# One Trainium2 core, one hybrid encoder layer: weights in column tiles from the host, and a fold without transposes

## The chip, the core and the metric

The kernel runs on one core of one Trainium2 chip. Its engines are TensorE (PE, with its weight loads PEld), VectorE (DVE), ScalarE (ACT), GpSimd (POOL) and SyncE (SP), which issues nearly all DMAs from one queue in order. The metric is the time of one execution on the device in microseconds (us); lower is better. A time is the median of a few runs. The profile is one execution of its own.

## The reference

One encoder layer on x of 2048 tokens by 1024, all in float32, with 256 memory tokens. Three sub-layers, each between two RMS norms:

```python
u = rms_norm(h, g_mix_pre);  z = u @ w_in                       # 1024 x 2816
ya = swa_with_sinks(qa, ka, va, sinks)                          # 8 heads of 64, window of chunks
yh = hgrn2(qh, fh, ih, gh, lb, onorm)                           # 4 heads of 128, gated recurrence
h = h + rms_norm(concat(ya, yh) @ w_out, g_mix_post)
u = rms_norm(h, g_x_pre);  m = rms_norm(mem, g_mem)
q, k, v = u @ wq, m @ wk, m @ wv                                # 4 heads of 256
h = h + rms_norm(softmax(q @ k.T / 16) @ v @ wo, g_x_post)
u = rms_norm(h, g_ffn_pre)
h = h + rms_norm((silu(u @ w_gate) * (u @ w_up)) @ w_down, g_ffn_post)   # 1024 x 2816, 2816 x 1024
```

## The kernel before

A float32 product is made from two parts of each operand in the type fp32r: hi, a rounded copy, and lo, what is left (raw - hi). Three matmuls stand for one: hi*hi, hi*lo, lo*hi (`mm3`, and `products` at L1002 to L1004). So every weight tile that is loaded (a raw tile) is first split: one copy makes hi and one subtraction on DVE makes lo. For the tiles of the `wp` pool this is `split`: hi on POOL at L142, lo on DVE at L143. `raw_tile` and `split_tiles` allot them, two buffers for each of raw, hi and lo, and `wcols` loads a block of 128 columns of a weight and splits it. A raw tile is 128 x 1024, 512 KB.

The stages, in the order of time:

- `in_first` projects the first half of the tokens with w_in; the weights stream through `streamed` (tiles `sraw`, in `in_block` two loads of 128 columns each for a half of the rows).
- `in_proj` / `in_cols` projects the second half, a block of 128 columns at a time (`wcols` of w_in), interleaved with `swa` and `hgrn` for the first half, whose input comes back from the DRAM tensor `z_d`.
- `fold_cross`, interleaved with the last `hgrn` blocks (L776 to L834 are theirs). It multiplies the cross-attention weights with the memory tokens once: k from w_k (`projected`, 8 tiles, 24 matmuls of 256 columns each), then for each of 8 row blocks of w_q the product with k (24 matmuls of 256 columns; the result is `qk_d`), then v from w_v (as k), then the product of v with w_o (8 tiles, 12 matmuls of 512 columns each; the result is `vo_d`). A row block of w_q has its model rows on the partitions and is needed the other way round: `transpose_split` transposes it on PE in eight blocks of 128 x 128 (L124) into two PSUM banks, which ACT and DVE take over as hi and lo (L126, L127). The other three weights go through `split`. PSUM banks here are of four kinds, g, t, s and h, two buffers each; the fold uses s and h.
- `phases` runs the rest from a list of jobs: out-projection (`mixed_block`), scores and values of the cross-attention, the FFN's gate and up (`hidden_blocks`, weights streamed with 256 columns a load) and down. Its products are 2 x 2 block products of seven multiplications instead of eight where the block's kind is "s"; `resident` prepares the operands T, `streamed` the operands S. Residual rows are added by DMAs that POOL issues (`add`, L1348); their descriptors lie in a ring in SBUF, whose size the program sets (`dynamic_dma_scratch_size`).

A scheduler in the build decides the order of the instructions on each engine from its own model of times; the engines then run their queues in order, and SP its DMAs. An instruction that waits holds up all behind it on its engine.

Of the kernel before, what the change touches and what calls it, by code (L numbers as in the profile page):

```python
# [24 lines left out]
KT = D // P  # L25
# [11 lines left out]
def f32(ap):  # L37
    return ap.bitcast(F32)
# [10 lines left out]
class Layer:  # L49
# [24 lines left out]
    def load(self, dst, src):  # L74
        self.nc.sync.dma_start(dst, src)
# [52 lines left out]

    def raw_tile(self):
        self._n += 1  # L130
        return self.wp.tile([P, D], F32, tag="raw", name=f"raw_{self._n}", bufs=2)

    def split_tiles(self):
        self._n += 1
        hi = self.wp.tile([P, D], F32R, tag="hi", name=f"whi_{self._n}", bufs=2)
        lo = self.wp.tile([P, D], F32R, tag="lo", name=f"wlo_{self._n}", bufs=2)
        return hi, lo

    def split(self, raw, hi, lo, lo_engine=None):

        nc = self.nc
        nc.gpsimd.tensor_scalar(hi, raw, 1.0, 1.0, ALU.mult, ALU.mult)  # L142
        (lo_engine or nc.vector).tensor_tensor(lo, raw, f32(hi), ALU.subtract)  # L143

    def wcols(self, w, c0, lo_engine=None):

        raw = self.raw_tile()
        self.load(raw.rearrange("p (k c) -> p k c", k=KT), w[:, c0:c0 + P].rearrange("(k p) c -> p k c", p=P))
        hi, lo = self.split_tiles()
        self.split(raw, hi, lo, lo_engine)  # L150
# [112 lines left out]
    def fold_cross(self):  # L263

        nc, ph = self.nc, self.xp
        gx = ph.tile([P, KT], F32, name="gx")
        self.load(gx, self.I["g_x_pre"].rearrange("r (k p) -> p (r k)", p=P))
        nc.vector.tensor_scalar_mul(gx, gx, float(M) ** -0.5)
        g = self.gain(self.I["g_mem"])
        mT = [ph.tile([P, KT, M], F32R, name=f"mT{i}") for i in range(2)]  # L270
        raw_tile, split_tiles = self.raw_tile, self.split_tiles

        def projected(w):
            dst = [ph.tile([P, KT, M], F32R, tag=f"kv{i}", name=f"kv{i}_{self._n}") for i in range(2)]
            for j in range(KT):
                wh, wl = self.wcols(w, j * P)
                ps = self.bank("sh"[j % 2])[:, :M]
                self.mm3(ps, [((wh[:, k, :], wl[:, k, :]), (mT[0][:, k, :], mT[1][:, k, :])) for k in range(KT)])
                nc.scalar.activation(dst[0][:, j, :], ps, AF.Copy)
                nc.vector.tensor_tensor(dst[1][:, j, :], ps, f32(dst[0][:, j, :]), ALU.subtract)  # L280
                yield dst

        for t in range(M // P):
            m = raw_tile()
            self.load(m, self.I["mem"][t * P:(t + 1) * P, :])
            u = self.pre_norm(m, g)
            self.transpose_split(u, lambda q: mT[0][:, 4 * q:4 * q + 4, t * P:(t + 1) * P],
                                 lambda q: mT[1][:, 4 * q:4 * q + 4, t * P:(t + 1) * P])
        for kT in projected(self.I["wk_x"]):
            yield  # L290
        for d in range(KT):
            wq = raw_tile()
            self.load(wq, self.I["wq_x"][d * P:(d + 1) * P, :])
            th, tl = split_tiles()
            th = th.rearrange("p (k c) -> p k c", k=KT)
            tl = tl.rearrange("p (k c) -> p k c", k=KT)
            self.transpose_split(wq, lambda q: th[:, 4 * q:4 * q + 4, :], lambda q: tl[:, 4 * q:4 * q + 4, :])
            o = self.io_tile("x")
            for q in range(2):
                ps = self.bank("sh"[q])  # L300
                for r in range(2):
                    h = 2 * q + r
                    self.mm3(ps[:, r * M:(r + 1) * M],
                             [((th[:, j, :], tl[:, j, :]), (kT[0][:, j, :], kT[1][:, j, :])) for j in (2 * h, 2 * h + 1)])
                sl = slice(q * 512, (q + 1) * 512)
                nc.scalar.activation(o[:, sl], ps, AF.Copy, scale=gx[:, d:d + 1])
            self.store(self.qk_d[d * P:(d + 1) * P, :], o)
            yield
        for vT in projected(self.I["wv_x"]):
            yield  # L310
        for h in range(4):
            banks = [[self.bank(k) for k in "sh"] for _ in range(2)]
            for i in range(2):
                j = 2 * h + i
                raw = raw_tile()
                self.load(raw, self.I["wo_x"][j * P:(j + 1) * P, :])
                wh, wl = split_tiles()
                self.split(raw, wh, wl)
                for mt in range(2):
                    ms = slice(mt * P, (mt + 1) * P)  # L320
                    ah, al = vT[0][:, j, ms], vT[1][:, j, ms]
                    for q in range(2):
                        sl = slice(q * 512, (q + 1) * 512)
                        nc.tensor.matmul(banks[mt][q], ah, wh[:, sl], start=(i == 0), stop=False)
                        nc.tensor.matmul(banks[mt][q], ah, wl[:, sl], start=False, stop=False)
                        nc.tensor.matmul(banks[mt][q], al, wh[:, sl], start=False, stop=(i == 1))
# [189 lines left out]
    def in_block(self, ca, cb, beside, get, between):  # L516

        nc, w = self.nc, self.I["w_in"]
        z, x = [], []

        def load(t, j):
            if between and j:
                between()
            for i, c in enumerate((ca, cb)):
                self.load(t[:, :, i * P:(i + 1) * P], w[j * 512:(j + 1) * 512, c * P:(c + 1) * P]
                          .rearrange("(k p) c -> p k c", p=P))

        def stream(kind):
            for n in beside:
                t = self.pair_tile()  # L530
                self.load(t[:, 0, :], self.I["x"][TB + n * P:TB + (n + 1) * P, :])
                x.append((n, t))
            for _ in range(3):
                next(iter(get), None)
            return self.streamed(load, 4, kind)

        def out(i, j, a, b):
            if not z:
# [19 lines left out]
        def after():  # L558
# [29 lines left out]
    def in_cols(self, b, u, cols, e1):  # L588
        nc = self.nc
        w = []  # L590
        for c in cols:
            w.append(self.wcols(self.I["w_in"], c * P))
# [20 lines left out]
        for i, c in enumerate(cols):  # L613
            c0 = c * P
# [269 lines left out]
    def resident(self, get, nk, key, dst, keep, sums):  # L884
# [70 lines left out]
    def streamed(self, load, nk, kind, engine=None):  # L955

        nc = self.nc
        raw = []
        for j in range(2):
            self._n += 1  # L960
            t = self.ts.tile([P, 4, 256], F32, tag="raw", name=f"sraw_{self._n}", bufs=self.raws)[:, :nk, :]
            load(t, j)
            raw.append(t)
        yield None
        a11, a21 = raw[0][:, :, 0:P], raw[0][:, :, P:2 * P]
        a12, a22 = raw[1][:, :, 0:P], raw[1][:, :, P:2 * P]

        def made(src, e):
            self._n += 1
# [523 lines left out]
    def down_block(self, c, f0, nk, n):  # L1493
# [51 lines left out]
        def after():  # L1545
# [44 lines left out]
```

## Time and profile before

| | before |
|---|---|
| runs | 2653.74, 2656.38, 2657.7 us, median 2656.38 |
| the profiled execution | span 2652.4 us from its first to its last instruction; the median of the runs is 4.0 us above it |
| PE busy | 2568.9 us, 97% of the span |
| DVE, ACT, POOL busy | 1714.9, 1240.2, 485.2 us |
| DMA | 494.48 MB, 186 GB/s on average |
| granted TensorE clock | 0.990 on average |

A busy PE is not PE at its peak: matmuls overlap, and their ends are modelled, so the distance between the starts of two of them says what one costs. In the windows below, the columns are the stretch, its length, then busy time and (instructions) of PE, PEld, DVE, ACT and POOL, the granted clock, the share of the 16 DMA engines and GB/s. The chain of waits gives start, length and what. A row of the waits gives who waited for whom, us in total, times, and the longest. A row of a tile gives shortest / median / longest in ns and the first and last start.

### The profile page before, as it was taken

To read this page: it belongs to the slowest core of one execution; us is meant where nothing else is said; L and a number is where in the kernel's file an instruction comes from. 1 tells how busy PE (TensorE), PEld (TensorE's weight loads), DVE (VectorE), ACT (ScalarE), POOL (GpSimd) and SP (SyncE) were. 2 spreads that over 40 slices of the span, in tenths; PEclk is the share of its full clock that TensorE was granted. 3 is DMA by queue.
4 is the path that set the end of the run, shared out by engine and by line. 5 is a ranking of instruction groups with operands and counts; after the bars stand their busy time and mean duration, and the time that the engine had idled before them with its cause. 6 is when DMAs were issued, how large, how long until landed. Compare 5 with 4: busy or idle time off the path is not lost.

```text
span 2652.4 us, 34824 instructions
## 1 busy us (share of the span) xinstructions
PE 2568.9 (97%) x12329; PEld 2145.1 (81%) x12329; DVE 1714.9 (65%) x2701; ACT 1240.2 (47%) x2604; POOL 485.2 (18%) x675
## 2 busy tenths in 40 slices
PE   7999999999988999999989999999999999999998
PEld 6877888888986877888878888888888888888886
DVE  7675578877545657777666655556666656564656
ACT  5463366655433556555564333344333334353543
POOL 4240344322432323223310000000000000001022
PEclk9999999999999999999999999999999999999999
DMA  5435655445877998676893633253566435576988
GB/s 183 144 130 165 191 156 159 131 140 171 233 234 222 276 296 266 210 238 176 220 307 126 192 120 95 80 182 127 168 198 211 162 108 171 173 232 173 264 214 215
DMA packets 405102, 494.48 MB, mean 186 GB/s; under 512 B 20416, under 2 KB 311232, under 8 KB 404928
## 3 DMA queue, kind: packets, MB, share of 16 engines
q1 hardware_dynamic: 394272, 453.46, 53.3%
q0 software_dynamic: 10656, 38.80, 8.3%
q8 instruction: 97, 1.59, 0.2%
q14 instruction: 77, 0.63, 0.1%
HBM read 333.85 MB, written 158.33 MB: 186 GB/s over the span
## 4 chain that ended last, share of the span: by engine, by line
PE 75%; DMA 10%; issue 7%; DVE 4%; POOL 3%; ACT 2%; SPq 0%; POOLq 0%; DVEq 0%; ACTq 0%
PE psm L1002 20%; PE psm L1004 20%; PE psm L1003 20%; PE psg L160 2%; PE psg L159 2%; PE psg L158 2%; PE pss L1237 1%; DMA row<-y_d 1%; DMA row<-in_w_out_dram 1%; DMA u_d<-row 1%; DMA raw<-in_wv_x_dram 1%; DMA raw<-in_wo_x_dram 1%; DVE wlo L143 1%; DMA row<-in_x_dram 1%; DMA pair<-in_x_dram 0%
## 5 line engine op out<-in xcount | busy, mean ns | idle before, releaser
L1002 PE MATMUL psm<-T,S 128*128 128x512 f32 x2699 | 1049.2, 393 | 19.9 <-ACT part L1017 6.9
L1003 PE MATMUL psm<-T,S 128*128 128x512 f32 x2699 | 1054.7, 391 | 5.7 <-DVE T L880 5.7
L1004 PE MATMUL psm<-T,S 128*128 128x512 f32 x2699 | 1046.4, 392 | 0.7 <-DVE S L880 0.6
L1002 PEld LDWEIGHTS psm<-T,S 128*128 128x128 f32 x2699 | 509.3, 189 | 132.3 <-ACT part L1017 8.2
L1003 PEld LDWEIGHTS psm<-T,S 128*128 128x128 f32 x2699 | 509.3, 189 | 111.8 <-DVE T L880 7.4
L1004 PEld LDWEIGHTS psm<-T,S 128*128 128x128 f32 x2699 | 509.2, 189 | 108.9 <-DVE S L880 3.1
L880 DVE TENSOR_TENSOR S<-sraw,S 128x512 fp32r<-128x512 f32 (+1 forms) x320 | 222.9, 703 | 213.3 <-ACT S L877 195.9
L877 ACT ACTIVATE S<-sum 128x512 fp32r<-128x512 f32 (+1 forms) x310 | 186.4, 619 | 342.5 <-PE psm L1004 244.3
L880 DVE TENSOR_TENSOR S<-sum,S 128x512 fp32r<-128x512 f32 (+1 forms) x368 | 248.5, 686 | 55.4 <-ACT S L877 35.7
L1017 ACT ACTIVATE part<-psm 128x512 f32<-128x512 f32 x270 | 160.0, 597 | 245.9 <-PE psm L1004 227.9
L1348 POOL DMA_DIRECT2D row<-y_d x28 | 25.7, 918 | 1127.4 <-DVE row L1521 1033.9
L877 ACT ACTIVATE S<-sraw 128x512 fp32r<-128x512 f32 (+1 forms) x273 | 168.0, 616 | 122.7 <-PE psm L1004 102.8
L880 DVE TENSOR_TENSOR T<-row,T 128x1024 fp32r<-128x1024 f32 (+1 forms) x122 | 144.2, 1195 | 63.8 <-ACT T L877 63.6
L158 PE MATMUL psg<-u,whi 128*128 128x512 f32 x352 | 141.3, 401 | 1.6 <-POOL whi L142 1.6
L160 PE MATMUL psg<-u,wlo 128*128 128x512 f32 x352 | 139.6, 397 | 0.9 <-DVE wlo L143 0.9
L159 PE MATMUL psg<-u,whi 128*128 128x512 f32 x352 | 139.4, 396 | 0.0
L877 ACT ACTIVATE T<-row 128x1024 fp32r<-128x1024 f32 x122 | 122.3, 1028 | 33.2 <-DVE row L906 17.9
L1319 ACT ACTIVATE junk<-row 128x512 f32<-128x512 f32 x160 | 99.9, 626 | 79.1 <-DVE row L1341 28.4
L879 POOL TENSOR_SCALAR S<-sum 128x512 fp32r<-128x512 f32 x58 | 50.2, 865 | 209.8 <-PE psm L1004 159.9
L977 DVE TENSOR_TENSOR sum<-sraw,sraw 128x512 f32<-128x512 f32 (+1 forms) x92 | 64.0, 696 | 32.0 <-DMA sraw<-h1t_d 8.7
L143 DVE TENSOR_TENSOR wlo<-raw,whi 128x1024 fp32r<-128x1024 f32 x46 | 60.3, 1311 | 36.1 <-POOL whi L142 36.1
L1472 DVE TENSOR_TENSOR row<-psm,part 128x512 f32<-128x512 f32 x63 | 41.7, 688 | 59.3 <-PE psm L1004 59.2
(332 smaller groups left out, 3622.0 us busy)
## 6 DMA issues: line engine op xcount, KB each, us to landing
sraw<-in_w_gate_dram SPq DMA_DIRECT2D x44, 512.0 KB, 3.9
sraw<-in_w_up_dram SPq DMA_DIRECT2D x44, 512.0 KB, 4.0
hid_d<-row SPq DMA_DIRECT2D x44, 512.0 KB, 2.6
h_d<-row SPq DMA_DIRECT2D x32, 512.0 KB, 5.8
y_d<-row SPq DMA_DIRECT2D x32, 512.0 KB, 3.1
sraw<-hid_d SPq DMA_DIRECT2D x32, 512.0 KB, 5.3
row<-h_d POOLq DMA_DIRECT2D x30, 512.0 KB, 6.5
row<-u_d SPq DMA_DIRECT2D x30, 512.0 KB, 6.3
```

Source lines behind the costliest of these rows:

```text
L143: (lo_engine or nc.vector).tensor_tensor(lo, raw, f32(hi), ALU.subtract)
L158: nc.tensor.matmul(ps, ah, bh, start=(i == 0), stop=False)
L159: nc.tensor.matmul(ps, ah, bl, start=False, stop=False)
L160: nc.tensor.matmul(ps, al, bh, start=False, stop=(i == n - 1))
L877: self.nc.scalar.activation(hi, raw, AF.Copy)
L880: self.nc.vector.tensor_tensor(lo, raw, f32(hi), ALU.subtract)
L977: nc.vector.tensor_tensor(t, a, b, op)
L1002: nc.tensor.matmul(ps, s[:, 0, k, :], t[:, 0, k, :], start=st, stop=False, **kw)
L1003: nc.tensor.matmul(ps, s[:, 0, k, :], t[:, 1, k, :], start=False, stop=False, **kw)
L1004: nc.tensor.matmul(ps, s[:, 1, k, :], t[:, 0, k, :], start=False, stop=sp, **kw)
L1017: nc.scalar.activation(t, ps, AF.Copy)
L1319: self.nc.scalar.activation(junk, a, AF.Square, scale=float(D) ** -0.5, accum_out=to)
```

## The change

- The host lays six weights (w_in, w_q, w_k, w_v, w_gate, w_up) out in tiles of 128 columns: tile c holds, for each partition, all eight row blocks of these columns in one run of 4 KB. w_q is transposed first. A raw tile of `wcols` is then one contiguous block of 512 KB; before, it was read in runs of 512 B. The streamed loads of w_in and of w_gate and w_up read runs of 2 KB; before, 512 B and 1 KB.
- In the fold, w_q goes through `wcols` like w_k, and its transposes and their take-over are gone.
- raw, hi and lo of the `wp` pool have three buffers instead of two. To make room for them, POOL's descriptor ring gets 2048 B of a partition instead of the default.
- `split` takes the engine of hi; in the fold hi is made by ACT (`"A"`), in the in-projection and for k of the attention still by POOL.

```diff
 def raw_tile:      tag="raw",   -bufs=2  +bufs=3
 def split_tiles:   tag="hi","lo" -bufs=2  +bufs=3
-    def split(self, raw, hi, lo, lo_engine=None):
+    def split(self, raw, hi, lo, engine="P"):
-        nc.gpsimd.tensor_scalar(hi, raw, 1.0, 1.0, ALU.mult, ALU.mult)
-        (lo_engine or nc.vector).tensor_tensor(lo, raw, f32(hi), ALU.subtract)
+        if engine == "A":
+            nc.scalar.activation(hi, raw, AF.Copy)
+        else:
+            nc.gpsimd.tensor_scalar(hi, raw, 1.0, 1.0, ALU.mult, ALU.mult)
+        nc.vector.tensor_tensor(lo, raw, f32(hi), ALU.subtract)
 def wcols:
-        self.load(raw.rearrange("p (k c) -> p k c", k=KT), w[:, c0:c0 + P].rearrange("(k p) c -> p k c", p=P))
+        self.load(raw, w[c])
 def fold_cross:
-                wh, wl = self.wcols(w, j * P)
+                wh, wl = self.wcols(w, j, "A")
-            wq = raw_tile()
-            self.load(wq, self.I["wq_x"][d * P:(d + 1) * P, :])
-            th, tl = split_tiles()
...
-            self.transpose_split(wq, lambda q: th[:, 4 * q:4 * q + 4, :], lambda q: tl[:, 4 * q:4 * q + 4, :])
+            th, tl = self.wcols(self.I["wq_x"], d, "A")
-                self.split(raw, wh, wl)
+                self.split(raw, wh, wl, "A")
 def in_block:
-                self.load(t[:, :, i * P:(i + 1) * P], w[j * 512:(j + 1) * 512, c * P:(c + 1) * P]
-                          .rearrange("(k p) c -> p k c", p=P))
+                self.load(t[:, i, :], w[c, :, j * 512:(j + 1) * 512])
 def streamed:  with tiled=True the two column blocks of a raw tile lie one behind the other
 def hidden_blocks:
-                t, w[j * 512:(j + 1) * 512, f * P:(f + 2) * P].rearrange("(k p) c -> p k c", p=P)), 4, kind, "A")
+                t, w[f:f + 2, :, j * 512:(j + 1) * 512].rearrange("i p d -> p i d")), 4, kind, "A", tiled=True)
+TILED = ("w_in", "wq_x", "wk_x", "wv_x", "w_gate", "w_up")
+def tiled(w):
+    return np.ascontiguousarray(w.reshape(KT, P, -1, P).transpose(2, 1, 0, 3)).reshape(-1, P, D)
 def kernel:
+        if name in TILED:
+            host[name] = tiled(host[name].T if name == "wq_x" else host[name])
-    nc = _bacc.Bacc("TRN2", target_bir_lowering=False, num_devices=1)
+    nc = _bacc.Bacc("TRN2", target_bir_lowering=False, num_devices=1, dynamic_dma_scratch_size=2048)
```

More of the change, by code (lines that the diff above doesn't have):

```diff
@@ L130, in raw_tile, with wcols @@
         self._n += 1
-        return self.wp.tile([P, D], F32, tag="raw", name=f"raw_{self._n}", bufs=2)
+        return self.wp.tile([P, D], F32, tag="raw", name=f"raw_{self._n}", bufs=3)
     def split_tiles(self):
         self._n += 1
-        hi = self.wp.tile([P, D], F32R, tag="hi", name=f"whi_{self._n}", bufs=2)
-        lo = self.wp.tile([P, D], F32R, tag="lo", name=f"wlo_{self._n}", bufs=2)
+        hi = self.wp.tile([P, D], F32R, tag="hi", name=f"whi_{self._n}", bufs=3)
+        lo = self.wp.tile([P, D], F32R, tag="lo", name=f"wlo_{self._n}", bufs=3)
         return hi, lo
-    def split(self, raw, hi, lo, lo_engine=None):
+    def split(self, raw, hi, lo, engine="P"):
         nc = self.nc
-        nc.gpsimd.tensor_scalar(hi, raw, 1.0, 1.0, ALU.mult, ALU.mult)
-        (lo_engine or nc.vector).tensor_tensor(lo, raw, f32(hi), ALU.subtract)
-    def wcols(self, w, c0, lo_engine=None):
+        if engine == "A":
[3 more added lines that the diff above has]
+        nc.vector.tensor_tensor(lo, raw, f32(hi), ALU.subtract)
+    def wcols(self, w, c, engine="P"):
         raw = self.raw_tile()
-        self.load(raw.rearrange("p (k c) -> p k c", k=KT), w[:, c0:c0 + P].rearrange("(k p) c -> p k c", p=P))
+        self.load(raw, w[c])
         hi, lo = self.split_tiles()
-        self.split(raw, hi, lo, lo_engine)
+        self.split(raw, hi, lo, engine)
         return (hi.rearrange("p (k c) -> p k c", k=KT), lo.rearrange("p (k c) -> p k c", k=KT))
@@ L291, in fold_cross @@
         for d in range(KT):
-            wq = raw_tile()
-            self.load(wq, self.I["wq_x"][d * P:(d + 1) * P, :])
-            th, tl = split_tiles()
-            th = th.rearrange("p (k c) -> p k c", k=KT)
-            tl = tl.rearrange("p (k c) -> p k c", k=KT)
-            self.transpose_split(wq, lambda q: th[:, 4 * q:4 * q + 4, :], lambda q: tl[:, 4 * q:4 * q + 4, :])
+            th, tl = self.wcols(self.I["wq_x"], d, "A")
             o = self.io_tile("x")
@@ L534, in stream @@
                 next(iter(get), None)
-            return self.streamed(load, 4, kind)
+            return self.streamed(load, 4, kind, tiled=True)
         def out(i, j, a, b):
@@ L591, in in_cols @@
         for c in cols:
-            w.append(self.wcols(self.I["w_in"], c * P))
+            w.append(self.wcols(self.I["w_in"], c))
         z = [self.io_tile("z") for _ in cols]
@@ L953, in mark, with streamed @@
             self.last[e] = next((i for i in reversed(traced) if i.engine == e), None)
-    def streamed(self, load, nk, kind, engine=None):
+    def streamed(self, load, nk, kind, engine=None, tiled=False):
         nc = self.nc
@@ L960, in streamed @@
             self._n += 1
-            t = self.ts.tile([P, 4, 256], F32, tag="raw", name=f"sraw_{self._n}", bufs=self.raws)[:, :nk, :]
-            load(t, j)
-            raw.append(t)
+            t = self.ts.tile([P, 4, 256], F32, tag="raw", name=f"sraw_{self._n}", bufs=self.raws)
+            if tiled:
+                t = t.rearrange("p k c -> p (k c)").rearrange("p (i d) -> p i d", i=2)
+                load(t, j)
+                raw.append([t[:, i, :].rearrange("p (k c) -> p k c", c=P) for i in range(2)])
+            else:
+                t = t[:, :nk, :]
+                load(t, j)
+                raw.append([t[:, :, i * P:(i + 1) * P] for i in range(2)])
         yield None
-        a11, a21 = raw[0][:, :, 0:P], raw[0][:, :, P:2 * P]
-        a12, a22 = raw[1][:, :, 0:P], raw[1][:, :, P:2 * P]
+        (a11, a21), (a12, a22) = raw
         def made(src, e):
```

## The prediction

> **What bounds the kernel now.** I read the page first (busy shares and the chain that ended last), then the windows by stage, then the chain, the waits and the DMA issues inside the one stage that the windows single out.
>
> ```profile
> span 2652.4 us, 34824 instructions
> PE 75%; DMA 10%; issue 7%; DVE 4%; POOL 3%; ACT 2%; SPq 0%; POOLq 0%; DVEq 0%; ACTq 0%
> 1500.00:1600.00 100.00, 100.00 (x443) 82.81 (x442) 58.22 (x88) 35.59 (x63) 0.00 (x0) 1.00 0.44 138
> 640.00:700.00 60.00, 54.24 (x396) 51.92 (x394) 36.84 (x47) 23.81 (x63) 25.20 (x25) 0.94 0.86 231
> 700.00:752.00 52.00, 49.39 (x410) 49.00 (x409) 21.89 (x38) 26.37 (x77) 16.57 (x23) 0.97 0.74 230
> 752.00:787.00 35.00, 26.85 (x195) 25.33 (x194) 17.43 (x24) 6.75 (x20) 14.56 (x13) 0.90 0.90 268
> 787.00:815.00 28.00, 26.00 (x124) 20.19 (x123) 11.67 (x11) 6.98 (x14) 8.41 (x8) 1.00 0.70 244
> ```
>
> The chain is 75% TensorE. The FFN window (1500 to 1600) shows what its floor is: 443 matmuls in 100 us, 0.226 us for each of 512 columns, with no idle time at all. There the weights of w_gate and w_up may arrive however they like, so their new layout is worth nothing and I cost it at 0. The fold of the cross-attention weights, 640 to 815, is different: PE idle, a granted clock below 1.00 in three of four windows, and DMA shares of 0.70 to 0.90. Almost all that this change can move lies in these 175 us. The built order of the changed kernel says the same: on SP it is that of before up to the first weights of the second in-projection (about 260 us) and again from the first w_out rows after the fold to the end.
>
> Inside the fold, this is how the weights come (the chain, start, length, what):
>
> ```profile
> 755.14 1.24 DVE wlo L143
> ...
> 767.70 1.23 DVE wlo L143
> 769.13 8.74 DMA raw<-in_wv_x_dram
> 778.04 1.06 POOL whi L142
> 779.12 1.24 DVE wlo L143
> 780.37 5.16 DMA raw<-in_wv_x_dram
> ...
> 813.22 1.24 DVE wlo L143
> ...
> 815.94 0.25 PE pss L326
> ```
> ```profile
> SPq L75 <- DVE wlo L143: 28.8, 13, 3.1
> ```
>
> It is a ring: load a raw tile, POOL makes hi, DVE makes lo, and only then is the raw tile free for the next load; SP, whose queue is in order, stands waiting for that release 13 times, 28.8 us in all. With two raw tiles one turn of the ring brings two weight tiles. From the wlo at 755.14 to that at 813.22 seven turns brought 14 tiles: 58.1 us, 8.3 us a turn, 4.15 us a tile.
>
> **The transposes that go.** Eight wq tiles lose eight transposes each, 64 PE instructions.
>
> ```profile
> 699.08 0.60 PE L124 MATMUL pss<-ident,raw 128*128 128x128 f32 x4
> 699.52 0.60 PE L124 MATMUL psh<-ident,raw 128*128 128x128 f32 x4
> 677.00 0.28 PE L159 MATMUL pss<-mT,whi 128*128 128x256 f32 x1
> 677.12 0.28 PE L160 MATMUL pss<-mT,wlo 128*128 128x256 f32 x1
> ```
>
> Four of them take 0.44 us from start to start, 0.11 each: 64 x 0.11 = 7.0 us. PE is the resource that is filled in the wq part (49.39 of 52 us busy), so I count all of it. Their PSUM banks and the hand-over through them go too. The sixteen half-tile evictions on ACT and DVE give way to eight whole hi copies on ACT and eight whole lo subtractions on DVE, the same columns: 0.
>
> **The third raw, hi and lo tiles.** In the wv part a tile is 24 matmuls of 256 columns at 0.12 us (the two rows above), 2.8 us; a wo tile is 12 of 512 columns at 0.226, 2.7 us. A turn of 8.3 us that brings three tiles gives 2.77 us a tile: just PE's pace. Sixteen tiles at 2.8 are 44 us against the 61 us that the two parts take (from the lo part at 755.14, with which the first wv products start, to the end of the wo products at 816.2), so the bound of the gain is 17. The other end comes from the DMA engines:
>
> ```profile
> DMA packets 14673, 16.22 MB, mean 257 GB/s; under 512 B 528, under 2 KB 12620, under 8 KB 14668
> raw<-in_wo_x_dram SPq DMA_DIRECT2D x8, 512.0 KB, 4.1
> raw<-in_wv_x_dram SPq DMA_DIRECT2D x7, 512.0 KB, 5.3
> 900.00:1000.00 100.00, 95.81 (x444) 76.81 (x443) 58.40 (x71) 51.27 (x119) 32.17 (x51) 1.00 1.01 300
> ```
>
> Between 752 and 815 16.22 MB move (the first row is that window's). At the 300 GB/s that the engines reach at a share of 1.01 these take 54 us, 9 less than the 63. The built order starts up to three wv loads before the last wq tiles are done, 1.5 MB or 5 us more that leave the window: 9 to 14. I take 12, nearer to the DMA bound than to PE's 17.
>
> **The wk and wq parts.** Two waits here belong to the ring:
>
> ```profile
> 681.66 0.38 PE L160 MATMUL psh<-mT,wlo 128*128 128x256 f32 x1 [1.59 <-DVE wlo L143]
> 679.00:682.00 3.00, 1.36 (x9) 0.96 (x8) 2.44 (x2) 2.23 (x10) 1.58 (x3) 1.00 1.08 285
> 682.00:685.00 3.00, 3.00 (x18) 3.00 (x17) 1.99 (x3) 1.08 (x2) 2.92 (x3) 0.57 0.68 192
> PE pst L792 <- issue: 2.4, 1, 2.4
> POOL qq L769 <- DMA qq<-z_d: 7.4, 2, 6.5
> 703.00:706.00 3.00, 2.77 (x14) 2.60 (x13) 2.52 (x6) 2.28 (x6) 1.66 (x2) 0.50 0.95 295
> ```
>
> PE waits 1.6 us for a wlo at 680, and 2.4 us at 700 in the HGRN's products, for which the profile names no releaser; just before it POOL's HGRN work had stood 6.5 us for a qq load, which SP had issued behind a wq load held by the ring. After each the clock falls: 0.57 and 0.50 over the next three microseconds, 1.3 and 1.5 us lost. Together 6.8 us. The first goes if wk tiles are split ahead; the second if SP no longer stops for the raw tile, of which I am less sure, since SP also waits for other tiles there. Bounds 0 and 6.8; I take 5.
>
> The Trainium skill, "TensorE: Matmul & The Clock Gate" (Why this matters for your kernels), asks for no PE idle gap over about 3 us if the clock is to stay up, so that by it a wait of 1.6 us costs no clock. The trace disagrees: 0.57 right behind a wait of 1.59. By the rule the two waits would be worth 4.0 and not 6.8, and the whole sum about 2 us less.
>
> **The hi parts on ACT.** 32 whole hi copies come to ACT, 24 of them from POOL (wk, wv, wo), 8 in place of the wq evictions.
>
> ```profile
> L142 POOL TENSOR_SCALAR whi<-raw x46: 1046/1052/2128, 264.1 to 812.1; 128x1024 fp32r<-128x1024 f32 x46
> L877 ACT ACTIVATE T<-row 128x1024 fp32r<-128x1024 f32 x122 | 122.3, 1028 | 33.2 <-DVE row L906 17.9
> POOL whi L142 <- DMA raw<-in_wo_x_dram: 15.5, 6, 4.1
> POOL whi L142 <- DMA raw<-in_wv_x_dram: 14.4, 5, 4.5
> POOL whi L142 <- DMA raw<-in_wk_x_dram: 6.3, 2, 3.4
> ```
>
> One costs 1.03 us there (the copies of the same shape at L877) against POOL's 1.05: the ring's turn is as long as before. ACT is busy 23.8 + 26.4 + 6.8 + 7.0 = 64 of these 175 us; 33 us more make 97, so it has room on average. What is queued behind each copy on ACT is what matters: the PSUM evictions of wk and wv (kv), of wq and wo (x) and of the HGRN blocks (atz, kt, vt), and PE waits for the banks that they empty. POOL spent 15.5 + 14.4 + 6.3 = 36 us waiting for raw tiles to land; a wait of that kind now stands in ACT's queue. With three tiles loaded ahead I expect it rarely: 0, and the other end is the slower rival. What POOL gains, it gains off the path.
>
> **The layout.** A wv tile, read in runs of 512 B, lands in 5.3 us, a wo tile, read in whole rows, in 4.1: at most 1.2 us a load, at the least none. Outside the fold two chain steps wait for such a load:
>
> ```profile
> 20.14 3.38 DMA sraw<-in_w_in_dram
> 260.52 4.90 DMA raw<-in_w_in_dram
> ```
>
> Between 0 and 2.4 us in all; I take 1. The Trainium skill, "DMA: Bandwidth & Descriptors" (Specifications), puts the line rate at 512 B and over, which w_in's runs already had. By that rule this term is 0 and the forecast 1 us later.
>
> **What is late next.** Behind the fold comes a second gap: w_out rows for the next resident tiles.
>
> ```profile
> 821.89 5.68 DMA row<-in_w_out_dram
> 848.61 1.15 DVE T L880
> ```
>
> Their loads stand on SP behind the last vo stores and need the fold's memory, so they move with the fold's end and take nothing back: 0. The smaller descriptor ring (2 KB instead of the default) serves POOL's adding loads alone; I cost it at 0 as they come in pairs.
>
> **Sum.** 7 + 12 + 5 + 1 = 25 us. Against the profiled execution's span: 2652.4 - 25 = 2627.4. The three runs were 2653.74 to 2657.7, their median 2656.38, 4.0 above that span; so 2631.4.
>
> **The rivals.**
>
> *The loads keep the pace (0.17).* Three loads in flight share the same engines, each lands later, and the turn grows with the tiles. For it: the share of 0.90 at 268 GB/s in the wv part, and a landing of 8.74 us. Against it: 0.70 in the wo part, where the ring and not the engines was slow. At 268 GB/s the 16.22 MB take 60.5 us, 2.5 less; with the transposes and 2 us of the waits, 2656.4 - 11.5 = 2645.
>
> *Nothing measurable (0.06).* The removed transposes lie in waits that stay, and the ring is paced by the loads as it is now: 2656, at most 5 us from before.
>
> *ACT is held by a tile that has not landed (0.08).* This one is slower. In wk and wv a hi copy stands ahead of a kv eviction; the banks s and h have two buffers each, so PE can run on for one product, 2.8 us, and a copy that waits longer stops it. The point from which it decides is thus a wait of ACT over 2.8 us on a raw tile. If half of POOL's 36 us of such waits become PE's and the ring gains nothing: 2656.4 + 18 - 7 = 2667. POOL's longest waits of that kind were 3.4 to 4.5 us, so the point is within reach. Against it: there were 13 of them on a ring of two, and the third tile lets a load start a whole turn earlier.
>
> *The short descriptor ring stalls POOL (0.03).*
>
> ```profile
> row<-h_d POOLq DMA_DIRECT2D x30, 512.0 KB, 6.5
> ```
>
> If each adding load had to wait until the one before has landed, 6.5 us, POOL's half of the S parts would come late in the 900 to 1390 stretch. 30 x 6.5 = 195 us of POOL time there, most of it in POOL's idle time; if a tenth reaches PE, +19.5 less the 25 of the fold leaves little, if a fifth does, 2656.4 + 39 - 25 = 2670.
>
> **How the numbers follow.** The forecast has 0.66. Its own ends: the transposes alone, 2649; and 7 + 17 + 6.8 + 2.4 = 33.2 with what the first two windows show lost besides: idle 5.8 + 2.6 less the 4.0 of the two waits, clock 0.06 x 60 + 0.03 x 52 = 5.2 less the 2.8 behind them, 6.8 more, 40 us, 2616. That range takes in the first rival (2645) and leaves out the last three, 0.17 together, and little of the forecast. About 0.2% (5 us) is what a measurement of this kernel can tell from no change: faster 0.83 (0.66 + 0.17), same 0.06, slower 0.11 (0.08 + 0.03).
>
> **What would show it.** Right: no L124 rows on raw tiles; the wv and wo parts, first to last product, in 46 to 52 us instead of 61; SP's waits for wlo well under 28.8 us; no PE wait over 3 us between 750 and 790; the FFN windows still 443 matmuls in 100 us. Wrong: wv and wo landings over 8 us with the parts still near 60 us (the first rival); ACT rows that wait for raw tiles for over 2.8 us with PE behind kv or x (the slower one); POOL's issuing of adding loads much longer than now (the last).

## The result, and the profile after

The changed kernel takes 2638.38 us in the median of 4 runs (2634.33 to 2640.89); the kernel before, run beside it, 2657.04 (2653.74 to 2665.44). The ratio is 0.9931, with a 95% interval of 0.9913 to 0.9949. Run again later in 5 runs, it took 2635.93, ratio 0.9943 (0.9930 to 0.9955). By the medians it is 18.7 us faster at first and 17.8 later, by the ratios 18 and 15, where 25 were forecast. The profiled execution is the run of 2634.33 us; its span is 2632.6, 19.8 less than that of before.

The page of the kernel after (span; TensorE's busy time, share and instructions; the chain by engine):

```profile
span 2632.6 us, 34672 instructions
PE 2555.3 (97%) x12265; PEld 2129.9 (81%) x12265; DVE 1712.0 (65%) x2693; ACT 1261.0 (48%) x2620; POOL 465.6 (18%) x651
PE 77%; DMA 11%; DVE 4%; ACT 3%; issue 3%; POOL 2%; SPq 0%; DVEq 0%; POOLq 0%; ACTq 0%
```

The windows of the kernel after: one of the FFN, then wk, wq, wv and wo. The columns are the window and its length, busy time of PE, PEld, DVE, ACT and POOL (with instructions), the granted clock, the DMA share and GB/s:

```profile
1500.00:1600.00 100.00, 100.00 (x443) 82.81 (x442) 58.66 (x89) 36.32 (x65) 0.00 (x0) 1.00 0.34 117
661.00:696.00 35.00, 34.15 (x281) 33.17 (x280) 25.02 (x32) 20.85 (x46) 11.50 (x11) 1.00 0.86 240
696.00:746.00 50.00, 45.40 (x375) 44.14 (x374) 21.60 (x31) 27.84 (x72) 21.50 (x24) 1.00 0.81 262
746.00:770.00 24.00, 24.00 (x206) 24.00 (x205) 13.10 (x18) 10.07 (x22) 3.38 (x5) 1.00 0.83 270
770.00:795.00 25.00, 23.93 (x102) 18.31 (x101) 12.65 (x15) 15.81 (x26) 0.00 (x0) 1.00 0.82 302
```

The same four parts of the kernel before, from its own first products on:

```profile
658.00:705.00 47.00, 41.61 (x320) 40.47 (x321) 29.83 (x39) 17.53 (x53) 23.84 (x25) 0.94 0.88 239
705.00:755.00 50.00, 49.06 (x414) 48.83 (x412) 19.92 (x34) 27.79 (x84) 14.96 (x20) 0.99 0.73 225
755.00:791.00 36.00, 28.79 (x209) 27.45 (x210) 19.25 (x24) 4.45 (x11) 14.69 (x14) 0.91 0.87 262
791.00:817.00 26.00, 24.00 (x99) 17.81 (x98) 9.56 (x9) 8.25 (x17) 7.35 (x7) 1.00 0.69 243
```

The FFN window has its 443 matmuls again. The wv part went from 36 us, of which PE worked 28.79 at a clock of 0.91, to 24 us without a gap at the full clock. The wq part tells the opposite: before, PE was busy 49.06 of 50 us; after, 39 matmuls are gone from it, it is just as long, and 4.6 us of it are idle.

For all that follows I measure two stretches from the rows of single products: **A**, from the first kk transposes of HGRN ahead of the fold to the first wv product, and **B**, from there to the end of the last wo product. A begins at the kk transposes and not at the first wk product because the third tiles move 20 HGRN matmuls from behind that product to ahead of it. Before: A 107.8 us (647.4 to 755.2), B 61.5 (to 816.6). After: A 98.3 (648.2 to 746.5), B 48.1 (to 794.6). So A gave 9.5 us and B 13.4, 22.8 together with rounding; 0.8 us went before A, and 2.3 after B (1835.7 to 1838.0 us from the last wo product to the end). In the fourteen traces of this study that last stretch lies between 1831.9 and 1838.6, without order by what the kernels change, so I read the 2.3 as spread between executions.

### The profile page after: what moved, and what is told of

Same layout as the page of the kernel before. It is cut to its first block, busy times and chain, and to the rows that moved or that the text cites. A ratio compares the mean times of both kernels' runs of the same rounds, so it can differ in the third digit from the quotient of the medians.

```text
span 2632.6 us, 34672 instructions
## 1 busy us (share of the span) xinstructions
PE 2555.3 (97%) x12265; PEld 2129.9 (81%) x12265; DVE 1712.0 (65%) x2693; ACT 1261.0 (48%) x2620; POOL 465.6 (18%) x651
## 4 chain that ended last, share of the span: by engine, by line
PE 77%; DMA 11%; DVE 4%; ACT 3%; issue 3%; POOL 2%; SPq 0%; DVEq 0%; POOLq 0%; ACTq 0%
PE psm L1004 21%; PE psm L1005 21%; PE psm L1006 21%; PE psg L163 2%; PE psg L161 2%; PE psg L162 2%; PE pss L1239 1%; DMA z<-in_w_out_dram 1%; DMA h1t_d<-row 1%; DMA row<-in_w_out_dram 1%; DMA u_d<-row 1%; DMA row<-y_d 1%; DMA row<-in_x_dram 1%; DMA row<-u_d 1%; DMA sraw<-in_w_in_dram 1%
## 5 line engine op out<-in xcount | busy, mean ns | idle before, releaser
L146 DVE TENSOR_TENSOR wlo<-raw,whi 128x1024 fp32r<-128x1024 f32 x54 | 68.5, 1269 | 26.0 <-ACT whi L143 18.1
L1474 DVE TENSOR_TENSOR row<-psm,part 128x512 f32<-128x512 f32 x63 | 41.7, 687 | 59.1 <-PE psm L1006 58.9
```

Source lines behind the costliest of these rows:

```text
L146: nc.vector.tensor_tensor(lo, raw, f32(hi), ALU.subtract)
```

## The experiments

Each run's ratio is to the runs of before taken beside it (medians there 2654.21, 2653.77 and 2654.19; 2657.04 for the first row of after). A and B come from the one profiled execution of each kernel.

What A and B can say is limited. A profiled execution need not be a typical one: it took 6.7 us more than the median of its kernel's runs for two_tiles and 4.9 more for pool_hi, 4.0 less for after, 6.8 less for no_transposes_alone and 7 less for after_two_kk_sg. And before and small_ring_alone, which the medians do not tell apart, differ by 1.1 us in A and 0.7 in B, so a difference of that size is no effect. The build also orders the instructions anew for each edit: 44 HGRN matmuls lie between the first kk transposes and the first wk product in every kernel with two tiles, 64 with three (68 in the last row). What a run shows is the edit together with its order.

| kernel | wq transposes | tiles | hi by | layout | median us | ratio (95%) | A | B |
|---|---|---|---|---|---|---|---|---|
| before | yes | 2 | POOL | rows | 2654.2 | 1 | 107.8 | 61.5 |
| small_ring_alone | yes | 2 | POOL | rows | 2656.23 | 1.0005 (0.9994-1.0016) | 106.7 | 60.8 |
| no_transposes_alone | no | 2 | POOL | rows | 2654.2 | 1.0004 (0.9994-1.0014) | 106.6 | 58.9 |
| act_hi_alone | yes | 2 | ACT | rows | 2651.72 | 0.9993 (0.9982-1.0004) | 102.4 | 63.6 |
| act_hi_no_transposes | no | 2 | ACT | rows | 2643.07 | 0.9962 (0.9950-0.9975) | 97.4 | 61.9 |
| two_tiles | no | 2 | ACT | tiles | 2641.38 | 0.9952 (0.9935-0.9970) | 97.5 | 59.7 |
| three_tiles_alone | yes | 3 | POOL | rows | 2641.12 | 0.9962 (0.9949-0.9975) | 105.4 | 52.5 |
| act_hi_three_tiles | yes | 3 | ACT | rows | 2641.7 | 0.9951 (0.9939-0.9962) | 101.4 | 49.8 |
| wq_transposes | yes | 3 | ACT | tiles | 2634.76 | 0.9921 (0.9904-0.9937) | 100.9 | 48.6 |
| pool_hi | no | 3 | POOL | tiles | 2637.0 | 0.9934 (0.9919-0.9950) | 101.9 | 47.0 |
| old_layout | no | 3 | ACT | rows | 2637.7 | 0.9937 (0.9915-0.9959) | 101.7 | 48.0 |
| after | no | 3 | ACT | tiles | 2638.38 | 0.9931 (0.9913-0.9949) | 98.3 | 48.1 |
| after_again | no | 3 | ACT | tiles | 2635.93 | 0.9943 (0.9930-0.9955) | 97.9 | 48.0 |
| after_two_kk_sg | no | 3 | ACT | tiles | 2631.02 | 0.9908 (0.9896-0.9921) | 95.0 | 46.2 |

**First set: the changed kernel with one part undone.**

*two_tiles*

```diff
-        return self.wp.tile([P, D], F32, tag="raw", name=f"raw_{self._n}", bufs=3)
+        return self.wp.tile([P, D], F32, tag="raw", name=f"raw_{self._n}", bufs=2)
...
-        hi = ... bufs=3)      # lo likewise
+        hi = ... bufs=2)
```

> The changed kernel with two raw, hi and lo buffers instead of three (the small descriptor ring stays), all else as changed. Theory A, the ring of weight tiles sets the pace of the wv and wo parts: they go back from 48 us towards the 61 us of before, SP's waits for wlo rise from 6.9 us towards 28.8, and the time is 10 to 15 us above the changed kernel's 2638 (ratio to before 0.997 to 1.000). Rival B, it was the move of hi to ACT or the layout that made these parts shorter: they stay under 52 us and the time within 4 us of 2638 (0.993).

B is 59.7 us again, and this is its window:

```profile
748.00:808.00 60.00, 52.21 (x302) 44.83 (x301) 26.42 (x32) 26.79 (x48) 4.69 (x5) 0.94 0.72 248
```

PE idles 7.8 us in it, at 0.94, while the DMA engines have room (0.72). The ring of two is what makes B long. But A stays at 97.5: something else owns most of A. Neither theory came out whole. B went back as theory A said, but the median is only 3 to 5 us above the changed kernel's, where theory A said 10 to 15 and rival B less than 4. The traces of this kernel and of after differ by 10.7 us in A and B together; but the one here, 2648.1 us, is the slowest of its four executions (the others took 2639.74 to 2641.75), and that of after is the fastest of its four. Beside the other parts the third tiles are thus worth 3 to 5 us in the medians; why not more, the traces do not show.

*pool_hi*

```diff
-                wh, wl = self.wcols(w, j, "A")
+                wh, wl = self.wcols(w, j)
...
-            th, tl = self.wcols(self.I["wq_x"], d, "A")
+            th, tl = self.wcols(self.I["wq_x"], d)
...
-                self.split(raw, wh, wl, "A")
+                self.split(raw, wh, wl)
```

> The changed kernel with every hi part of the fold on POOL again. Theory A: the ring's turn is as long (1.05 us a copy on either engine) and three tiles cover it, so the wv and wo parts stay within 3 us of 48 and the time within 4 us of 2638; the wq part may even get shorter, because the x evictions on ACT no longer stand behind hi copies. Rival B, ACT is what made the parts shorter (POOL is held up by DVE's two-input subtractions and by the HGRN's own work): 8 us or more slower than 2638, most of it in the wk and wq parts.

2637.0, with three tiles no different from the change. SP waits longer for wlo (window 640 to 805 of this kernel):

```profile
SPq L75 <- DVE wlo L146: 18.8, 11, 3.6
```

against 6.9 us after, but B is as short (47.0): the third tile covers POOL's copies in the wv and wo parts. A is 3.6 us longer. The median does not show this; the profiled execution is the slowest of its four.

*old_layout*

```diff
-        self.load(raw, w[c])
+        self.load(raw.rearrange("p (k c) -> p k c", k=KT), w[:, c * P:(c + 1) * P].rearrange("(k p) c -> p k c", p=P))
...
-        if name in TILED:
-            host[name] = tiled(host[name].T if name == "wq_x" else host[name])
+        if name == "wq_x":
+            host[name] = np.ascontiguousarray(host[name].T)
```

(and the streamed w_in, w_gate and w_up by rows, as before)

> The changed kernel with the host layout of before for w_in, w_k, w_v, w_gate and w_up (runs of 512 B and 1 KB), w_q transposed by the host but not laid out in tiles, so its column blocks are read in runs of 512 B too. Theory A, the landing hardly depends on the run length (5.3 against 4.1 to 5.4 us before): 1 to 3 us slower than 2638 (ratio 0.993 to 0.994). Rival C, the longer runs are what shortened the fold: wv landings well over 6 us, the wv and wo parts at 54 us or more, the time 8 us or more above 2638.

2637.7: with the weights by rows nothing is lost that the medians can tell. In its trace A is 3.4 to 3.8 us longer than in the two of the changed kernel, and the rest after the fold 2.4 to 4.2 shorter (1833.8 us against 1838.0 and 1836.2), so one trace does not settle it either.

*wq_transposes* (wq by rows again, out of the host's list of tiled weights)

```diff
-            th, tl = self.wcols(self.I["wq_x"], d, "A")
+            wq = raw_tile()
+            self.load(wq, self.I["wq_x"][d * P:(d + 1) * P, :])
+            ...
+            self.transpose_split(wq, lambda q: th[:, 4 * q:4 * q + 4, :], lambda q: tl[:, 4 * q:4 * q + 4, :])
```

> The changed kernel with w_q by rows and its 64 transposes on PE again, with their take-over as hi and lo; the third tiles, ACT's hi parts of the other weights and the layout stay. Theory A, the transposes cost what they take on PE: 7 us, the time 2645, the wq part 7 us longer than 50 us. Rival D, the wq part is paced by its waits (they rose by 4 us where the work fell by 4): 0 to 3 us slower than 2638.

2634.76: 64 transposes are back and the time is not longer. Its window of the wq part:

```profile
704.00:750.00 46.00, 46.00 (x396) 45.98 (x395) 19.99 (x33) 25.39 (x71) 12.99 (x18) 1.00 0.74 232
```

PE works without a gap here, where the changed kernel idles 4.6 of 50 us. The transposes filled time that their removal leaves empty: for their 7 us of work A is only 3 us longer.

**Second set: one part alone.** The four runs above all kept most of the gain, so each part was tried by itself, beside the changed kernel.

*after_again* (no edit)

> The changed kernel as it is, as the mark for the three runs beside it. 2638 us, 2634 to 2642; wk and wq parts (first wk product to first wv product) 84 to 89 us, wv and wo parts 47 to 50.

*three_tiles_alone*

```diff
-        return self.wp.tile([P, D], F32, tag="raw", name=f"raw_{self._n}", bufs=2)
+        return self.wp.tile([P, D], F32, tag="raw", name=f"raw_{self._n}", bufs=3)
...
-        hi = ... bufs=2)      # lo likewise
+        hi = ... bufs=3)
...
-    nc = _bacc.Bacc("TRN2", target_bir_lowering=False, num_devices=1)
+    nc = _bacc.Bacc("TRN2", target_bir_lowering=False, num_devices=1, dynamic_dma_scratch_size=2048)
```

> The kernel before with the third raw, hi and lo tiles (and the 2 KB descriptor ring that makes room for them), all else as before: transposes, POOL's hi parts, rows. If the parts of the change add up as predicted, the wv and wo parts go from 61 to about 49 us, the wk part loses its wait for the wlo, and the wq part keeps its transposes: wk and wq about 92, time about 2641. If the two parts overlap, because the HGRN blocks and not PE's work set the pace of wk and wq once their weights come in time, the third tiles alone bring wk and wq to 86 to 89 as well: about 2636, no slower than the whole change.

2641.12, as the adding-up theory said (2641), and not the 2636 of the overlap theory: B falls from 61.5 to 52.5, A only from 107.8 to 105.4. In the measure of the expectation, first wk to first wv product, it takes 89.3 us, which is nearer to the 86 to 89 of the overlap theory than to 92; that measure leaves out the 20 HGRN matmuls that move ahead of wk.

*no_transposes_alone*

```diff
-            wq = raw_tile()
-            self.load(wq, self.I["wq_x"][d * P:(d + 1) * P, :])
-            ...
-            self.transpose_split(wq, lambda q: th[:, 4 * q:4 * q + 4, :], lambda q: tl[:, 4 * q:4 * q + 4, :])
+            th, tl = self.wcols(self.I["wq_x"], d * P)
...
+        if name == "wq_x":
+            host[name] = np.ascontiguousarray(host[name].T)
```

> The kernel before with wq transposed by the host and its 64 transposes gone, two tiles of each kind, POOL's hi parts and rows as before. If the parts add up: wk and wq 97 - 7 = 90, wv and wo still about 60, time about 2648. If they overlap: wk and wq 86 to 89 too, wv and wo about 60, time about 2645. If the transposes lay in waits that stay: wk and wq 95 or more, time 2654.

1.0004: by itself the removal of 7 us of TensorE work is worth nothing that 12 runs can tell (0.9994 to 1.0014). Its wq part (window 701 to 754), its PE waits in 700 to 755 and, in 701 to 754, the group of POOL's hi copies (mean ns, then POOL's idle time before them):

```profile
701.00:754.00 53.00, 48.51 (x374) 47.19 (x375) 25.98 (x33) 20.80 (x64) 29.16 (x32) 0.94 0.83 251
PE pss L158 <- POOL whi L142: 3.7, 2, 2.0
L142 POOL TENSOR_SCALAR whi<-raw 128x1024 fp32r<-128x1024 f32 x10 | 10.4, 1043 | 1.9 <-PE psh L159 1.8
```

Without the transposes the hi parts of wq come to POOL too, into the same queue as HGRN's kk and q: 10 copies, 10.4 us, in this window. PE now waits 3.7 us for hi parts, where before it waited for none in the wk and wq parts. From the first wk to the first wv product all its waits together rise from 5.6 to 10.3 us, which takes back most of the work saved. The clock is not part of it: between these two products it stands at 0.50 for 6.8 us in both kernels. A fell by 1.2 us in this trace, of an execution that is the fastest of its 12.

*small_ring_alone*

```diff
-    nc = _bacc.Bacc("TRN2", target_bir_lowering=False, num_devices=1)
+    nc = _bacc.Bacc("TRN2", target_bir_lowering=False, num_devices=1, dynamic_dma_scratch_size=2048)
```

> The kernel before with the 2 KB descriptor ring alone. Costed at 0: 2654 to 2657, all parts as before. If it is the ring that gave the time, since it is the one part that all runs so far share: about 2640. If it stalls POOL's adding loads: above 2662.

1.0005: the ring neither gives nor costs.

**Third set: ACT's hi parts, and what is left of A.** Two tiles with neither transposes nor POOL's hi parts had taken 2641, without transposes alone 2654. Two things that could matter differ between them, ACT and the layout; the small ring gives nothing by itself.

*act_hi_alone*

```diff
-        nc.gpsimd.tensor_scalar(hi, raw, 1.0, 1.0, ALU.mult, ALU.mult)
+        if engine == "A":
+            nc.scalar.activation(hi, raw, AF.Copy)
...
-                wh, wl = self.wcols(w, j * P)
+                wh, wl = self.wcols(w, j * P, "A")
...
-                self.split(raw, wh, wl)
+                self.split(raw, wh, wl, "A")
```

> The kernel before with the hi parts of wk, wv and wo made by ACT, and nothing else: two tiles, wq transposes, rows. As predicted (a hi copy takes as long on ACT, and what POOL gains lies off the path): 0, so about 2654, wk and wq 97, wv and wo 61. If POOL's queue was the hidden bound of wk and wq (in the trace of before its hi copies there wait 16 us for raw tiles and for PE to free hi tiles, and the kk and q work of the HGRN blocks stands behind them): wk and wq 87 to 92, wv and wo 61, time about 2646.

0.9993, an interval that holds 1: A falls by 5.4 us in its trace, B does not, and the medians can't tell 2.5 us from none. The 2646 of the POOL theory did not come.

*act_hi_no_transposes* (the edits of act_hi_alone and of no_transposes_alone, the wq hi parts on ACT too)

> The kernel before with the hi parts on ACT and wq transposed by the host (so without the 64 transposes), two tiles, all weights still by rows. It differs from the run without transposes alone (2654) only in ACT's hi parts, and from the run with two tiles (2641) only in the layout. If POOL's queue was the bound: about 2641, wk and wq 86. If the layout made those 13 us: about 2654, wk and wq 95.

2643.07, 11 us below the run that differs from it only in the engine of the hi parts. The layout is out of it (two_tiles 2641.38). Its wq part and the only PE wait in 695 to 745:

```profile
696.00:744.00 48.00, 45.57 (x378) 44.36 (x378) 23.22 (x32) 27.77 (x72) 19.63 (x22) 1.00 0.91 277
PE pst L790 <- DVE on L823: 2.2, 2, 1.1
```

The waits for hi are gone and the clock is full. So with two tiles the removed transposes are worth 8.7 us (2651.72 to 2643.07) if the hi parts that take their place do not go through POOL's queue, and 0 if they do.

*act_hi_three_tiles* (the edits of act_hi_alone and of three_tiles_alone)

> The kernel before with three tiles of each kind, the 2 KB ring and hi parts on ACT: no change of layout, nothing done by the host, wq's 64 transposes kept. If transposes and layout are worth nothing once the tiles come in time and POOL is out of the ring: 2635 to 2638, as the whole change. By the prediction's terms (transposes 7, layout 1): about 8 us above the whole change, 2644.

2641.7, nearer to the 2644 of the prediction's terms than to the changed kernel's 2635.93; but wq_transposes, which has the tiled layout besides, took 2634.76. Their A and B differ by 0.5 and 1.2 us. With the host's work and without it the two pairs (this one, and old_layout against after) give 7 us and about 0 for the layout, in runs taken at different times. Of the 7 us the fold has 1.7 in the traces. That is not settled.

*after_two_kk_sg*

```diff
-        kk = get(new("kk"), C_FH)
+        kk = get(new("kk", 2), C_FH)
...
-        sg = ph.tile([P, 4, P], F32, tag="sg", name=f"sg{n}")
+        sg = ph.tile([P, 4, P], F32, tag="sg", name=f"sg{n}", bufs=2)
```

> The changed kernel with two buffers instead of one for the HGRN blocks' kk and sg tiles. wk and wq take 85 us in the changed kernel, of which 76 are PE's work and 8 are lost. If what is left of the loss is the HGRN blocks' loads standing behind SP's waits for the stores of sg, 22 us in that stretch: wk and wq 78 to 82, time about 2632. If the blocks are paced by their own chain through POOL, DVE, PE and ACT: 85 as before, time 2634 to 2640.

2631.02, the fastest of all: 0.9908 (0.9896 to 0.9921) against the changed kernel's 0.9943 (0.9930 to 0.9955) to the same kernel before, in runs taken one after the other. In the kernel after, two loads of kk lie on the chain of the whole program:

```profile
702.57 5.76 DMA kk<-z_d
727.13 5.33 DMA kk<-z_d
```

and this is what POOL's kk line waits for in 640 to 755, first in the kernel after, then with two buffers, with the latter's window of the wq part:

```profile
  DMA kk<-z_d: 15.4, 6
```
```profile
  DMA kk<-z_d: 9.3, 5
698.00:744.00 46.00, 45.86 (x384) 45.18 (x383) 22.70 (x32) 27.78 (x72) 19.35 (x21) 1.00 0.86 283
```

From the first wk product to the first wv product it takes 80.3 us instead of 85.4, inside the 78 to 82 expected of the load theory; PE idles 0.14 us of 46 in wq, against 4.6 of 50. The last four kk steps come every 10.8 to 11.5 us instead of 11.3 to 13.3. A load of kk is now issued a step ahead: that for the step at 734.5 us at 714.4, where in the kernel after that for the step at 737.3 was issued at 727.1.

That kk's load is what paces these steps is argued, not shown. In after_again, the same kernel as after, POOL's kk line waits as long in the same stretch, but for two releasers:

```profile
  PE psg L773: 11.0, 2
  DMA kk<-z_d: 4.4, 3
```

In the two steps put down to a PE product the load had landed 0.1 and 0.4 us before POOL's step began, so there an earlier load alone would have gained little. The 9.3 us above are of six steps, the 15.4 of seven, and the order of the instructions differs too. SP's waits for the stores of sg are hardly shorter (655 to 755: 20.5 us against 23.8 and 22.3 in the two traces of after), so I think it is kk's buffer; the two were not tried apart.

## Why the prediction was right, and where it was not

**The place.** It said that all of the gain lies in the fold. The two stretches gave 22.8 us, 24 were forecast for them.

**The third tiles: right.** 12 forecast, 13.4 measured in B for the whole change, near the DMA bound and not PE's 17; the third tiles alone take 9.0 off B. In all six traces with two tiles B is 58.9 to 63.6 us, in all eight with three 46.2 to 52.5. That B is not the whole of the time is said at two_tiles. What was to show it, after in 630 to 800, then PE's longest wait before in 750 to 820 and after in 740 to 800:

```profile
SPq L75 <- DVE wlo L146: 6.9, 8, 2.2
SPq L78 <- ACT x L330: 13.1, 7, 3.6
```
```profile
PE psh L158 <- POOL whi L142: 3.7, 1, 3.7
PE pss L323 <- DVE wlo L146: 0.9, 1, 0.9
```

SP's waits for wlo fell from 28.8 us to 6.9; in the ring's place it now stands 13.1 us for the output rows that ACT hands it to store, with loads enough ahead. No PE wait of 3 us is left. B is 48.1 us, inside the 46 to 52 named.

**The loads keep the pace: refuted.** A wv load lands as fast as before and a wo load 1.2 us later (issue to landing, median), both far from the 8 us named, at 302 GB/s in the wo part:

```profile
raw<-in_wv_x_dram SPq DMA_DIRECT2D x8, 512.0 KB, 5.2
raw<-in_wo_x_dram SPq DMA_DIRECT2D x8, 512.0 KB, 5.3
row<-h_d POOLq DMA_DIRECT2D x30, 512.0 KB, 6.4
```

**The ring stalls POOL: refuted**, by the last row (6.5 before) and by small_ring_alone.

**ACT held by a tile: refuted.** ACT's waits for raw tiles, 630 to 800 after, and its hi copies:

```profile
ACT whi L143 <- DMA raw<-in_wo_x_dram: 2.5, 3, 1.2
ACT whi L143 <- DMA raw<-in_wv_x_dram: 2.3, 1, 2.3
L143 ACT ACTIVATE whi<-raw x32: 1042/1058/1088, 611.8 to 788.3; 128x1024 fp32r<-128x1024 f32 x32
```

2.3 us at most, short of the 2.8 from which it decided, and the copy takes 1.06 us, where 1.03 was forecast.

**The transposes: the step that failed.** "PE is the resource that is filled in the wq part (49.39 of 52 us busy), so I count all of it." The 7 us of work went; in the traces less than half of that followed. With the rest of the change but the transposes kept (wq_transposes) A is already down from 107.8 to 100.9, mostly by waits and clock. Taking them out brings A to 98.3: counted as in the paragraph on the waits below, from the first wk to the first wv product the matmuls' own time falls from 82.4 to 76.5 us, and the time lost rises from 5.4 to 8.9. Full is not the same as bounding: the wq products are interleaved with HGRN's steps, and when PE's own work shrinks, PE waits at these steps instead. The changed kernel waits at these steps (690 to 745 after):

```profile
PE pst L789 <- DVE on L822: 2.8, 2, 1.9
PE pst L789 <- issue: 1.7, 1, 1.7
```

Two runs show that the term of 7 was wrong for this kernel: wq_transposes puts the work back without loss in the median, and no_transposes_alone gains nothing. It is not wrong everywhere: with two tiles and ACT's hi parts the same removal gave 8.7 us. Which part of HGRN's way (its loads, POOL, DVE, ACT) comes due is open; after_two_kk_sg, with A shorter by another 3 and the median by 5, points to kk's load. "What is late next" was asked behind the fold, and not here. Half of the rival of 0.06, that the removed transposes lie in waits that stay, thus came true; its other half, a ring paced by the loads, did not.

**Hi on ACT at 0: right with three tiles (pool_hi), wrong with two.** "What POOL gains, it gains off the path" doesn't hold where POOL has one queue for HGRN and the ring: ACT was worth 11 us beside the removed transposes. In the whole change the parts seem to overlap: by the medians third tiles alone gave 13 us, transposes and ACT together 11, all three 18; by the ratios 10, 10 and 15 to 18, each within 3 to 5 us. That there is an overlap is likely, its size is not shown. The terms were added as if each stood alone.

**The waits at 680 and 700: partly.** 5 were forecast. Counting every matmul at its undisturbed start-to-start time (0.108, 0.162, 0.117 and 0.226 us for 128, 192, 256 and 512 columns), the time between first wk and first wv product that isn't such work fell from 11.8 us to 8.9: 2.9. The two waits went, but others at HGRN's steps came, and PE's waits in this stretch are 5.3 us in all where they were 5.6. What went is the clock's share: before, it stood at 0.50 for 6.8 us of the stretch, which costs 3.4; after, it stays at 1.00. For the clock behind the new waits, after has these rows, two PE starts with the idle time before them and the windows that follow:

```profile
699.99 0.63 PE L789 MATMUL pst<-ident,v 128*128 128x128 f32 x4 [1.67 <-issue]
736.64 0.66 PE L789 MATMUL pst<-ident,v 128*128 128x128 f32 x4 [1.91 <-DVE on L822]
701.00:704.00 3.00, 3.00 (x28) 3.00 (x27) 1.63 (x4) 1.60 (x5) 1.65 (x2) 1.00 0.92 260
737.00:740.00 3.00, 3.00 (x27) 2.80 (x26) 2.01 (x4) 1.23 (x4) 1.96 (x1) 1.00 0.87 284
```

Behind waits of 1.67 and 1.91 us the clock stayed at 1.00, where before it fell to 0.57 behind 1.59. The Trainium skill, "TensorE: Matmul & The Clock Gate" (Why this matters for your kernels), lets gaps below about 3 us cost no clock; these two rows agree with it, those of before do not, and the length of the last wait alone does not decide it (last section).

**The layout: 1 forecast, nothing measurable** for the changed kernel (old_layout). By the Trainium skill's "DMA: Bandwidth & Descriptors" (Specifications) it was 0; the pair of runs agrees, the other pair (7 us, in runs taken at different times) leaves it open.

**The sum.** Of 25, the parts of the fold gave 22.8 in the profiled executions, and 3.1 went elsewhere. That the total was near is partly luck: B gave 1.4 more than its 12 and A 9.5 of its 12, and in A the gain came by another way than the sum: most of it is there with the transposes kept.

## What to carry to other kernels

A busy engine in an interleaved stretch isn't yet its bound: before its work is counted as gain, ask which chain on the other engines would be late if that work were gone, and try it alone. When a change joins several parts that feed one wait, price them in pairs: here one part was worth nothing alone and 8.7 us beside another. Where copies for a prefetch ring share an in-order queue with a recurrent chain, try a free engine for the copies and one more buffer for the chain's own load: here they gave 11 us (beside the removed transposes) and about 5, less work on the busy engine nothing by itself.

## What was not expected of the hardware

The granted clock: 0.57 and 0.50 behind waits of 1.59 and 2.4 us before, 1.00 behind 1.67 and 1.91 us after. The clock records in the fourteen traces show what separates the two. In each the clock changes only on a grid of 3.41 us, and only between 1.00 and 0.50. Here are stretches of that grid, first of before (each of the two waits, and the stretch that follows it), then of after (the wait of 1.67 us, then the wait of 1.91 us, which lies across two stretches):

```profile
679.03:682.44 3.41, 1.77 (x13) 1.37 (x12) 2.88 (x2) 2.67 (x10) 1.99 (x3) 1.00 0.97 257
682.44:685.86 3.42, 3.42 (x18) 3.42 (x17) 2.41 (x4) 0.64 (x2) 3.34 (x4) 0.50 0.69 194
699.51:702.92 3.41, 1.03 (x10) 0.79 (x8) 1.21 (x3) 0.00 (x0) 2.00 (x4) 1.00 0.64 179
702.92:706.34 3.42, 3.19 (x16) 2.94 (x15) 2.94 (x6) 2.37 (x6) 1.66 (x2) 0.50 0.94 292
```
```profile
698.43:701.85 3.42, 1.86 (x15) 1.72 (x16) 2.66 (x4) 0.26 (x1) 2.02 (x2) 1.00 0.87 286
732.57:735.98 3.41, 2.15 (x18) 1.95 (x16) 0.09 (x1) 0.69 (x1) 2.81 (x4) 1.00 0.56 199
735.98:739.39 3.41, 2.75 (x22) 2.56 (x23) 3.03 (x5) 0.62 (x3) 1.96 (x1) 1.00 0.68 234
```

PE was busy for 52% and 30% of the stretches that a half clock followed, and for 54%, 63% and 81% of the others. Over all fourteen traces, without their first 40 and last 15 us, there are 10420 stretches at full clock. Of the 78 in which PE was busy for under 40%, all were followed by a half clock; of the 10287 with 55% or more, none; of the 55 between, 24. So it is PE's busy share of such a stretch that goes with the fall, and where a wait lies on the grid matters as much as its length. This is a count over traces; no run varied it alone.
